# Adaptive average pooling on one core: the sum of each tile moved from GpSimd and VectorE to VectorE alone, and the last tile cut in two

## The chip, the cores and the metric

The kernel runs on one core of one Trainium2 chip. A core has engines that work side by side: VectorE (DVE in the profile), ScalarE (ACT), GpSimd (POOL), TensorE (PE, not used here) and SyncE (SP), which here only issues DMA transfers. Sixteen DMA engines move data between the memory (HBM) and the core's on-chip buffer of 128 partitions. The metric is the device time of one execution in microseconds (us). Before the change it is 333.39 us, the median of 3 runs (333.32 to 333.48).

## The reference

The input `x` is float32, 32 x 256 x 4096; the output is 32 x 256 x 256. With 4096 columns and 256 outputs every window has exactly 16 columns:

```python
for i in range(output_size):
    start = int(i * length / output_size)
    end = int((i + 1) * length / output_size)
    result[:, :, i] = np.mean(x[:, :, start:end], axis=-1)
```

So 8192 rows of 4096 numbers become 8192 rows of 256 means: 134.22 MB are read and 8.39 MB written, and there is one addition for each number read.

## The kernel before

The 8192 rows are worked in 16 tiles. A tile gives each of the 128 partitions 4 whole rows, 16384 numbers (64 KiB), in all 8.39 MB. `cells` = 1024 is the number of outputs of a tile in each partition, `cols` = 16384 the number of inputs, `window` = 16, and `m` = 512 is half of `cells`.

Tiles 0 to 14 are read from `x_many`, and their results stay on the chip in `res_many` until all 15 are there; one store of 7.86 MB then writes them. Tile 15 has its own source `x_last` and result `res_last`, which is written with two small stores: 120 partitions, then 8.

The input buffers come from `inpool`, which has two. The load of tile t can be issued only when tile t-2, which had the same buffer, has been summed. All DMA transfers are issued by SyncE, in the order of the program: SP's queue holds the 16 loads (L73), behind the last load the large store (L58 by way of `store`), then the two small stores. An instruction that waits on this queue holds back everything behind it.

For each tile the engines do this:

- L73: SyncE issues the load.
- L76: GpSimd adds, for the second half of the cells, the upper 8 columns of each window onto the lower 8, in place.
- L81: VectorE sums the first half of the cells, 16 columns for each (128 x 8192 numbers in, 128 x 512 out). It does not wait for GpSimd and runs beside it.
- L84: VectorE sums the second half of the cells, for which 8 columns are left (128 x 4096 in, 128 x 512 out). It waits for L76.
- L87: ScalarE multiplies the tile's 1024 results in place by 1/16.

The two buffers and the waits between the engines are handled by the framework's pool; the stores carry a semaphore of their own, on which SyncE waits at the end (L99).

Of the kernel before, what the change touches and what calls it, by code (L numbers as in the profile page):

```python
# [1 line left out]

# [4 lines left out]


@with_exitstack
def kernel(  # L10
    ctx: ExitStack,
    tc: tile.TileContext,
    x: bass.AP,
    output_size: int,
    out: bass.AP,
):

    nc = tc.nc
    F32 = mybir.dt.float32
    X = mybir.AxisListType.X

    batch, channels, length = x.shape
    ob, oc, olen = out.shape
    assert ob == batch and oc == channels and olen == output_size
    assert length % output_size == 0
    window = length // output_size  # L30
    hw = window // 2
    inv_w = 1.0 / float(window)

    P = nc.NUM_PARTITIONS
    R = 4
    rows = batch * channels
    assert rows % (P * R) == 0
    ntiles = rows // (P * R)
    many = (ntiles - 1) * R
    cells = R * output_size  # L40
    m = cells // 2
    cols = R * length

    xr = x.rearrange("b c l -> (b c) l")
    orow = out.rearrange("b c o -> (b c) o")
    x_many = xr[0 : P * many, :].rearrange("(p r) l -> p (r l)", p=P, r=many)
    o_many = orow[0 : P * many, :].rearrange("(p r) o -> p (r o)", p=P, r=many)
    x_last = xr[P * many :, :].rearrange("(p r) l -> p (r l)", p=P, r=R)
    o_last = orow[P * many :, :].rearrange("(p r) o -> p (r o)", p=P, r=R)

    res_many = nc.alloc_sbuf_tensor("res_many", [P, (ntiles - 1) * cells], F32, align_bytes=256)
    res_last = nc.alloc_sbuf_tensor("res_last", [P, cells], F32, align_bytes=256)
    inpool = ctx.enter_context(tc.tile_pool(name="inpool", bufs=2))

    stored = nc.alloc_semaphore("stored")

    def store(out, in_):
        ins = nc.sync.dma_start(out=out, in_=in_)  # L58
        tc.no_tile_sem_insts.add(ins.ins.name)
        ins.then_inc(stored, 16)  # L60

    for t in range(ntiles):
        last = t == ntiles - 1
        xbuf = inpool.tile([P, cols + 64], F32, name="xin")
        off = 32 if last else 0
        flat = xbuf[:, off : off + cols]
        xin = flat.rearrange("p (o w) -> p o w", w=window)
        if last:
            res, base, src = res_last, 0, x_last
        else:  # L70
            res, base = res_many, t * cells
            src = x_many[:, t * cols : (t + 1) * cols]
        nc.sync.dma_start(out=flat, in_=src)  # L73
        if last:
            store(o_many, res_many[:, :])
        nc.gpsimd.tensor_add(  # L76
            out=xin[:, m:cells, 0:hw],
            in0=xin[:, m:cells, 0:hw],
            in1=xin[:, m:cells, hw:window],
        )  # L80
        nc.vector.reduce_sum(  # L81
            out=res[:, base : base + m], in_=xin[:, 0:m, :], axis=X
        )
        nc.vector.reduce_sum(  # L84
            out=res[:, base + m : base + cells], in_=xin[:, m:cells, 0:hw], axis=X
        )
        nc.scalar.mul(  # L87
            out=res[:, base : base + cells],
            in_=res[:, base : base + cells],
            mul=inv_w,  # L90
        )
    for lo, hi in ((0, 120), (120, P)):
        store(o_last[lo:hi, :], res_last[lo:hi, :])

    ctx.pop_all().close()
    tc.close()
    tc.compile()  # L97
    nc.sync.wait_ge(stored, 48)
    nc.sync.sem_clear(stored)  # L99


# [1 line left out]
_INS = ['x', 'output_size']  # L103
_OUTS = [((32, 256, 256), 'float32')]

_NUMBERS = {'output_size': 256}


# [26 lines left out]
```

## Time and profile before

| | |
|---|---|
| median of 3 runs | 333.39 us |
| span of the profiled execution (first to last instruction) | 332.2 us |
| VectorE busy | 209.7 us, 63% |
| GpSimd busy | 139.7 us, 42% |
| ScalarE busy | 18.2 us, 5% |
| DMA packets' time, as a share of 16 engines' span | 99.4% |
| bytes moved | 142.61 MB, 429 GB/s over the span |
| GpSimd's add, 128x4096, each | 8719 ns |
| VectorE's sum, 128x8192, each | 8686 ns |
| VectorE's sum, 128x4096, each | 4420 ns |
| ScalarE's scaling, 128x1024, each | 1056 ns |

The profile records one execution, and its page gives the span from the first to the last instruction of that execution. It holds no other time of that execution; the median of the runs is 1.2 us above the span. "Landing" of a DMA transfer is the moment from which an engine that waits for its data can go on. A row of the timeline gives the start, the length, the engine, the line, the operation and its tile, and in brackets the idle time before it with what ended it. A row of the table of windows gives the window, its length, the busy time of VectorE, ScalarE and GpSimd with the number of instructions, TensorE's clock, the mean busy share of the DMA engines and their GB/s.

### The profile page before, as it was taken

What the parts mean: (1) busy time and instruction counts of PE and PEld (TensorE: products, weight loads), DVE (VectorE), ACT (ScalarE), POOL (GpSimd) and SP (SyncE); (2) the same over time, 40 slices, a digit from 0 to 9 for tenths busy, and PEclk for the clock granted to TensorE, in tenths of its full rate; (3) what the DMA queues carried; (4) which work ended last, traced back from release to release, by engine and by line L of the source; (5) the groups of instructions that cost most, each with busy time, mean ns of one, the idle gap of its engine ahead of it and who ended that gap; (6) DMA issues with size and microseconds to landing.
All of it is one profiled execution on the core that took longest, in us unless ns stands there. A gap on an engine that the chain in (4) does not pass through costs nothing.

```text
span 332.2 us, 160 instructions
## 1 busy us (share of the span) xinstructions
DVE 209.7 (63%) x32; ACT 18.2 (5%) x17; POOL 139.7 (42%) x20
## 2 busy tenths in 40 slices
DVE  0029396692939669392956939295683929578392
ACT  1000101000010100001010000101000010101001
POOL 0027090642709064370906337090633709063370
DMA  9898989989898999989898998989899998989897
GB/s 379 379 505 379 505 379 442 442 379 505 379 505 379 481 402 402 481 379 505 379 497 387 466 418 379 505 379 505 379 489 395 418 466 379 505 379 505 363 473 300
DMA packets 2599, 142.61 MB, mean 429 GB/s; under 512 B 295, under 2 KB 295, under 8 KB 423
## 3 DMA queue, kind: packets, MB, share of 16 engines
q1 hardware_dynamic: 2599, 142.61, 99.4%
HBM read 134.22 MB, written 8.39 MB: 429 GB/s over the span
## 4 chain that ended last, share of the span: by engine, by line
DMA 66%; POOL 18%; DVE 11%; POOLq 3%; issue 0%; ACT 0%; SPq 0%
DMA xin<-in_x_dram 66%; POOL xin L76 18%; DVE res_many L84 9%; POOLq L97 3%; DVE res_last L84 1%; ACT res_last L87 0%; SPq L73 0%; POOLq L76 0%
## 5 line engine op out<-in xcount | busy, mean ns | idle before, releaser
L76 POOL TENSOR_TENSOR xin<-xin 128x4096 f32<-128x4096 f32 x16 | 139.5, 8719 | 181.9 <-DMA xin<-in_x_dram 181.9
L81 DVE TENSOR_REDUCE res_many<-xin 128x512 f32<-128x8192 f32 x15 | 130.3, 8686 | 107.3 <-DMA xin<-in_x_dram 107.3
L84 DVE TENSOR_REDUCE res_many<-xin 128x512 f32<-128x4096 f32 x15 | 66.3, 4420 | 2.5 <-POOL xin L76 2.3
L87 ACT ACTIVATE res_many<-res_many 128x1024 f32<-128x1024 f32 x15 | 15.8, 1056 | 289.6 <-DVE res_many L84 289.6
L81 DVE TENSOR_REDUCE res_last<-xin 128x512 f32<-128x8192 f32 x1 | 8.7, 8686 | 6.6 <-DMA xin<-in_x_dram 6.6
L84 DVE TENSOR_REDUCE res_last<-xin 128x512 f32<-128x4096 f32 x1 | 4.4, 4420 | 0.2 <-POOL xin L76 0.2
L87 ACT ACTIVATE res_last<-res_last 128x1024 f32<-128x1024 f32 x1 | 1.1, 1056 | 18.8 <-DVE res_last L84 18.8
L87 ACT ACT_TABLE_LOAD x1 | 1.3, 1283 | 0.7 <-PEq L116 0.7
L116 POOL MEMSET const-float32-0.0<- 128x1 f32 x1 | 0.1, 99 | 0.2 <-issue 0.2
L116 POOL MEMSET const-bfloat16-1.0<- 128x1 bf16 x1 | 0.1, 102 | 0.0
L116 POOL MEMSET const-uint8-127<- 128x1 uint8 x1 | 0.1, 102 | 0.0
L116 POOL MEMSET const-float32-1.0<- 128x1 f32 x1 | 0.1, 99 | 0.0
## 6 DMA issues: line engine op xcount, KB each, us to landing
out_dram<-res_many SPq DMA_DIRECT2D x1, 7680.0 KB
out_dram<-res_last SPq DMA_DIRECT2D x1, 480.0 KB
xin<-in_x_dram SPq DMA_DIRECT2D x16, 25.3
out_dram<-res_last SPq DMA_DIRECT2D x1, 32.0 KB
```

Source lines behind the costliest of these rows:

```text
L76: nc.gpsimd.tensor_add(out=xin[:, m:cells, 0:hw], in0=xin[:, m:cells, 0:hw], in1=xin[:, m:cells, hw:window],)
L81: nc.vector.reduce_sum(out=res[:, base : base + m], in_=xin[:, 0:m, :], axis=X)
L84: nc.vector.reduce_sum(out=res[:, base + m : base + cells], in_=xin[:, m:cells, 0:hw], axis=X)
L87: nc.scalar.mul(out=res[:, base : base + cells], in_=res[:, base : base + cells], mul=inv_w,)
L97: tc.compile()
L116: nc = _bacc.Bacc("TRN2", target_bir_lowering=False, num_devices=1)
```

## The change

GpSimd's add (L76) is removed. Each tile is summed by one instruction of VectorE over all 1024 cells with 16 columns each, and scaled by one instruction of ScalarE as before. The last tile is treated as two column halves (`parts` = 2): two loads of 128 x 8192 numbers one after the other on SP's queue, each with its own sum and its own scaling. The large store is still issued behind the loads of the last tile, and the small stores at the end.

```diff
+    def sums(xin, res, base, count):
+        nc.vector.reduce_sum(out=res[:, base : base + count], in_=xin, axis=X)
+        nc.scalar.mul(
+            out=res[:, base : base + count],
+            in_=res[:, base : base + count],
+            mul=inv_w,
+        )
+
     for t in range(ntiles):
...
         if last:
-            res, base, src = res_last, 0, x_last
+            res, base, src, parts = res_last, 0, x_last, 2
         else:
-            res, base = res_many, t * cells
+            res, base, parts = res_many, t * cells, 1
             src = x_many[:, t * cols : (t + 1) * cols]
-        nc.sync.dma_start(out=flat, in_=src)
+        pc, pm = cols // parts, cells // parts
+        for k in range(parts):
+            nc.sync.dma_start(
+                out=flat[:, k * pc : (k + 1) * pc], in_=src[:, k * pc : (k + 1) * pc]
+            )
         if last:
             store(o_many, res_many[:, :])
-        nc.gpsimd.tensor_add(
-            out=xin[:, m:cells, 0:hw],
-            in0=xin[:, m:cells, 0:hw],
-            in1=xin[:, m:cells, hw:window],
-        )
-        nc.vector.reduce_sum(
-            out=res[:, base : base + m], in_=xin[:, 0:m, :], axis=X
-        )
-        nc.vector.reduce_sum(
-            out=res[:, base + m : base + cells], in_=xin[:, m:cells, 0:hw], axis=X
-        )
-        nc.scalar.mul(
-            out=res[:, base : base + cells],
-            in_=res[:, base : base + cells],
-            mul=inv_w,
-        )
+        xin = flat.rearrange("p (o w) -> p o w", w=window)
+        for k in range(parts):
+            sums(xin[:, k * pm : (k + 1) * pm, :], res, base + k * pm, pm)
```

More of the change, by code (lines that the diff above doesn't have):

```diff
@@ L30 @@
     window = length // output_size
-    hw = window // 2
     inv_w = 1.0 / float(window)
@@ L40 @@
     cells = R * output_size
-    m = cells // 2
     cols = R * length
@@ L66 @@
         flat = xbuf[:, off : off + cols]
-        xin = flat.rearrange("p (o w) -> p o w", w=window)
         if last:
-            res, base, src = res_last, 0, x_last
+            res, base, src, parts = res_last, 0, x_last, 2
         else:
-            res, base = res_many, t * cells
+            res, base, parts = res_many, t * cells, 1
             src = x_many[:, t * cols : (t + 1) * cols]
-        nc.sync.dma_start(out=flat, in_=src)
+        pc, pm = cols // parts, cells // parts
[3 more added lines that the diff above has]
+            )
         if last:
             store(o_many, res_many[:, :])
-        nc.gpsimd.tensor_add(
-            out=xin[:, m:cells, 0:hw],
-            in0=xin[:, m:cells, 0:hw],
-            in1=xin[:, m:cells, hw:window],
-        )
-        nc.vector.reduce_sum(
-            out=res[:, base : base + m], in_=xin[:, 0:m, :], axis=X
-        )
-        nc.vector.reduce_sum(
-            out=res[:, base + m : base + cells], in_=xin[:, m:cells, 0:hw], axis=X
-        )
-        nc.scalar.mul(
-            out=res[:, base : base + cells],
-            in_=res[:, base : base + cells],
-            mul=inv_w,
-        )
+        xin = flat.rearrange("p (o w) -> p o w", w=window)
+        for k in range(parts):
+            sums(xin[:, k * pm : (k + 1) * pm, :], res, base + k * pm, pm)
     for lo, hi in ((0, 120), (120, P)):
```

## The prediction

> **What bounds the kernel now.** I read the busy and DMA shares of the page first, then the chain that ended last, then the load line, then windows and the timeline at both ends.
>
> Page, parts 1 to 3:
>
> ```profile
> DVE 209.7 (63%) x32; ACT 18.2 (5%) x17; POOL 139.7 (42%) x20
> ...
> DMA  9898989989898999989898998989899998989897
> ...
> q1 hardware_dynamic: 2599, 142.61, 99.4%
> ```
>
> No engine is near full, the 16 DMA engines are: their packets fill 99.4% of the span. The kernel is bound by moving 142.61 MB, and any change can only lose by making the DMA engines wait, or win a little where the transfers start and end.
>
> The chain, two tiles of its middle (start, length, what):
>
> ```profile
> 80.68 8.73 POOL xin L76
> 89.41 0.02 issue
> 89.43 4.43 DVE res_many L84
> 93.86 0.02 issue
> 93.88 25.29 DMA xin<-in_x_dram
> 119.17 0.03 issue
> ```
>
> This is the circuit of one of the two input buffers: landed, summed (13.3 us), reload issued, 25.3 us to landing. It closes every 38.6 us, in which two tiles land. It does not show who is the bound: of the 25.3 us a part is waiting behind the other buffer's load. That is in the load line's times to landing:
>
> ```profile
> L73 SPq DMA_DIRECT2D xin<-in_x_dram x16: 327/328/420, 0.7 to 287.1; - x16
> ...
> DMA to landing us min/median/max: 21.8/25.3/40.6
> ```
>
> 21.8 us is the first load, which found idle queues; the median queued behind another. In the timeline two landings are one load's transfer apart: VectorE starts at 273.78 and 293.08, 19.30 us, 8.39 MB at 434 GB/s. So an unqueued load is 19.3 us of transfer and about 2.5 us of start and landing, and the median waits 25.3 - 21.8 = 3.5 us behind its neighbour. That 3.5 us is what the kernel has to spare per buffer circuit.
>
> The end, from the timeline and a table of windows:
>
> ```profile
> 293.08 8.69 DVE L81 TENSOR_REDUCE res_many<-xin 128x512 f32<-128x8192 f32 x1 [6.02 <-DMA xin<-in_x_dram]
> ...
> 306.40 1.06 ACT L87 ACTIVATE res_many<-res_many 128x1024 f32<-128x1024 f32 x1 [18.25 <-DVE res_many L84]
> 307.48 0.35 SPq L58 DMA_DIRECT2D out_dram<-res_many  x1
> 312.96 8.69 DVE L81 TENSOR_REDUCE res_last<-xin 128x512 f32<-128x8192 f32 x1 [6.59 <-DMA xin<-in_x_dram]
> ```
>
> ```profile
> 326.27 1.06 ACT L87 ACTIVATE res_last<-res_last 128x1024 f32<-128x1024 f32 x1 [18.81 <-DVE res_last L84]
> 327.35 0.74 SPq L58 DMA_DIRECT2D out_dram<-res_last  x2
> ```
>
> ```profile
> 1.17:22.16 20.99, 0.00 (x0) 0.84 (x1) 0.00 (x0) 1.00 1.06 446
> ...
> 60.84:292.76 231.92, 157.26 (x24) 12.67 (x12) 104.62 (x12) 1.00 1.00 434
> 292.76:312.56 19.80, 13.11 (x2) 1.06 (x1) 8.72 (x1) 1.00 1.00 421
> 312.56:330.20 17.64, 13.11 (x2) 1.06 (x1) 8.72 (x1) 1.00 0.91 394
> ```
>
> The large store (7.86 MB, 18.1 us at 434 GB/s) is issued 5 us before the last load is through and follows it without a gap; the last tile's arithmetic ends at 327.33 under that store. The end too is transfer time.
>
> **The change part by part.**
>
> *GpSimd's add goes.* 16 instructions of 8.72 us (POOL). In each tile it stands between landing and VectorE's second sum.
>
> *VectorE sums the tile whole.* The two rows give the price: 128x8192 takes 8686 ns, 128x4096 takes 4420 ns, so 4096 more elements cost 4266 ns (1.042 ns each) over a fixed 154 ns. 16384 elements: 154 + 17064 = 17.22 us. Bounds: 17.06 without a fixed part, 17.37 by doubling the 8686 row. The 8686 row ran beside GpSimd and the 4420 row did not, and one line goes through both with a small fixed part, so I see nothing for VectorE to gain from GpSimd's absence. VectorE goes from 209.7 to about 276 us, 83% of the span, still under the 19.3 us per tile.
>
> *The buffer circuit.* From landing to reload issued: before 13.3 us (50.63 + 4.43 less the start at 41.83, and 0.02), after 17.22 + 0.03 = 17.25 us. That takes 3.9 or 4.0 us out of a reserve of 3.5 us. In full: a reload issued 17.25 us after landing, and landing 21.8 us after its issue if its start is like the first load's, closes the circuit in 39.05 us. Two transfers need 38.6. The longer one sets the pace: +0.4 us for two tiles. The circuit is run through seven times by each buffer from the first landings to tiles 14 and 15, and both buffers' circuits run at the same time: 7 x 0.4 = 2.9 us. The first load's issue took 0.40 us on SP's queue, the later ones 0.33; with that 0.07 taken off, 7 x 0.34 = 2.4 us. I take 2.4.
>
> The unknown is what a reload costs that arrives when the DMA engines are just running dry, since before none did. From below: nothing, if its start lies beside the neighbour's last packets. The nearest fact on that is this table of the first load's start:
>
> ```profile
> 1.13:1.70 0.57, 0.00 (x0) 0.57 (x1) 0.00 (x0) 1.00 0.00 0
> 1.70:2.20 0.50, 0.00 (x0) 0.31 (x1) 0.00 (x0) 1.00 5.83 1966
> ```
>
> The last two columns are the DMA engines' busy share and GB/s. Packets are counted where they start: 1966 GB/s in 0.5 us are 15 packets of 65,536 bytes, so 15 of 16 DMA engines start within 1.0 to 1.4 us of the issue at 0.73. But in the packet records those first packets last about 3.05 us and all later ones 2.418, so the pipe also fills for some 0.6 us; that the fill hides behind a neighbour's packet is open. From above: the whole 21.8 us with a sum of 17.37 us, 7 x 0.56 = 3.9 us. I take the first load's row because it is the same transfer, queue and tile; only its neighbour differs.
>
> *The last tile's two halves.* Two loads of 4.19 MB in place of one; the second is issued some 0.35 us behind the first on SP's queue and transfers behind it, so it adds nothing. SP's order is kept: both loads, then the large store, which waits for ScalarE on tile 14. That wait grows: tile 14 lands at 293.08, is summed at 310.30, scaled (1.06 us) at 311.4; the store is issued at 311.4 in place of 307.48. Before, the 5 us of load still queued covered its start. Now the last load's transfer ends at about 312.1 to 312.6 and the store's bytes start at 311.4 plus between 1.0 us (the table above) and 2.1 us (21.8 less 19.3 of transfer less 0.4 from the last packet to VectorE's start): 312.4 to 313.5 against 312.6 before, or -0.1 to +0.9. I take +0.7, near the upper end, since the store meets empty queues, like the first load. What waits behind it on SP's queue are the two small stores.
>
> *The last sums.* VectorE is now late: tile 14 until 310.3, then two halves of 8.69 us until 327.7 (both halves landed long before). ScalarE on 128x512 is between half of 1.06 and all of it; say 0.6. The small stores are issued at 328.4, 1.0 later than before. The large store covers this: with its 18.1 us it now ends at about 331, and 328.4 + 2.1 = 330.5. If it started at 312.4 the cover would be gone and the small stores would add up to 0.1. Stall shifts both alike.
>
> *GpSimd's queue* loses its waits; no one else waited for it. ACT gets one instruction more, at the end, counted above.
>
> **The sum.** The profiled span is 332.2; the median of the runs, 333.39, lies 1.2 above it, which I keep as what lies around the span. 332.2 + 2.4 + 0.7 = 335.3, plus 1.2: 336.5 us. Of the DMA engines' time, the 3.1 us are new gaps.
>
> **The rivals.**
>
> *The reload's start is hidden anyway.* If a reload only has to be issued some 1.4 us before the neighbour ends, 17.25 + 1.4 + 19.3 + 0.4 = 38.35 is under 38.6 and the pace stays 19.3 per tile. Only the store's late start is left: 333.39 - 0.1 to + 0.9, so 333.3 to 334.3, 334.0 at my value. For it: descriptors reach 15 of 16 engines in that time. Against it: the long first packets, and the one engine whose first packet starts at 2.84. The Trainium skill, DMA: Bandwidth & Descriptors, Anatomy of one DMA, fits a fixed 2.0 us plus bytes at 436 GB/s, for GpSimd-issued DMAs: 21.2 us for this load by estimate, against the 21.8 measured here on SP's queue. By it the circuit is 38.5 us, just inside the two transfers, and this rival would hold, with a time of 334.0. The measured row outweighs it, but the difference is only 0.6 us in 39.
>
> *The reload starts later than the first load did*, because the queues and the memory are busy. At 1 us more, the circuit is 40 us and the loss 7 x 1.4 = 9.8: with the store's 0.7, 343.9 us. For it: the first load had the memory to itself. Against it: nothing here shows a start under load that takes longer; the issue itself gets shorter, 0.33 for 0.40.
>
> *Faster: the transfers speed up without GpSimd's reads and writes of the tile.* The price is the load's 19.3 us. The window of the first load, without any engine at work, has 446 GB/s against 434 later; at that rate a load is 18.8. It decides only where the circuit follows: 17.25 + start + 18.8 must be under 38.6, so a start under 2.55 us, which the first load's 2.5 barely meets; with a start of 1.4 the two transfers bind at 37.6 and the kernel gains 7 x 1.0, less 0.7: 327.1 us. Against it: the 446 comes from counting packets where they start, and packets last 2.418 us with and without GpSimd at work.
>
> **How the numbers follow.** Two runs of this kernel can be told apart by about 0.2%, 0.67 us. Start not hidden, as summed: 0.65, 334.3 to 338.4 (the lower end for a stall of 0.1 us a circuit, the upper for 3.9 us of stall and 0.9 at the store with 0.2 for the rest). Hidden: 0.23, 333.3 to 334.3, of which about 0.13 lies within 0.67 us of 333.39. Later start: 0.08. Faster: 0.04. Range 333.6 to 338.5, which leaves out the last two and the lowest part of the second. Slower: 0.65 + 0.10 + 0.08 = 0.83; same 0.13; faster 0.04.
>
> **What would show it.** Sums of 128x16384 at 17.2 us; time from load to landing with a median near 21.8 instead of 25.3; VectorE starts 19.5 us apart from tile to tile; VectorE waiting about 2.3 us for each load; DMA share below 99% in the middle; the store issued near 314; the small stores still not on the path. Starts 19.3 apart with a DMA share of 1.00 in the middle would show the first rival; starts 20 apart or more the second; starts below 19.2 the third. The prediction is wrong if a reload's start overlaps its neighbour's last packets, or if the sum is not linear in its elements.

## The result, and the profile after

The changed kernel takes 349.94 us (median of 4 runs, 348.85 to 352.37) against 333.44 us for the kernel before on the same chip: 1.050 times as long, 95% interval 1.048 to 1.053. Forecast were 336.5 us and at most 338.5. The sign was right, the size was five times too small.

The profiled execution took 352.37 us and has a span of 351.1 us, 18.9 us more than the span of before; it is the slowest of the four, and the medians differ by 16.5 us. From its page, the busy times, the DMA engines' digits, the queue and the sums:

```profile
DVE 275.5 (78%) x17; ACT 18.4 (5%) x18; POOL 0.2 (0%) x4
...
DMA  8989999997999899989989899898989979999995
...
q1 hardware_dynamic: 2743, 142.61, 96.1%
...
L61 DVE TENSOR_REDUCE res_many<-xin 128x1024 f32<-128x16384 f32 x15 | 258.3, 17220 | 67.9 <-DMA xin<-in_x_dram 67.9
```

A whole sum takes 17.22 us, as worked out. VectorE is still no bound: it waits 67.9 us for loads. But the DMA engines, with the same bytes, fell from 99.4% to 96.1%. They have gaps, and the chain of work that ended last shows where (start, length, what):

```profile
39.73 24.16 DMA xin<-in_x_dram
63.89 0.02 issue
63.91 17.23 DVE res_many L61
81.14 0.02 issue
81.16 24.20 DMA xin<-in_x_dram
...
122.64 23.86 DMA xin<-in_x_dram
...
163.77 22.05 DMA xin<-in_x_dram
...
203.09 24.66 DMA xin<-in_x_dram
...
245.02 24.55 DMA xin<-in_x_dram
...
286.84 22.09 DMA xin<-in_x_dram
```

The chain now goes round one buffer without any part hidden: sum 17.25 us, reload, sum. Two reloads took about the 21.8 us from issue to landing that the prediction used. The other five took 23.9 to 24.7. Before, such numbers cost nothing since they held 3.5 us of waiting behind the other buffer's load. Here most engines have next to nothing to wait for: by the packet records the first DMA engine through with the other load ran dry, that is, had no packet left to move, 1.3 us after the issue at the latest, in four of the seven cases before it. (The records hold the start, length and size of each packet of the trace, but not its engine. Which engine went on or stood empty is inferred from packets that start where another ends.)

From VectorE's start on tile 0 to its start on tile 14, the seven circuits add up to 308.95 - 22.48 = 286.5 us, against 293.08 - 22.53 = 270.6 before: 15.9 us lost. The other 3.0 of the 18.9 us lie behind tile 14 (351.1 - 308.95 = 42.1, before 332.2 - 293.08 = 39.1). The stores there:

```profile
327.29 0.35 SPq L56 DMA_DIRECT2D out_dram<-res_many  x1
...
344.05 1.62 SPq L56 DMA_DIRECT2D out_dram<-res_last  x2
```

What a slow reload looks like is seen in windows around the one issued at 39.73, and for comparison around the quick one issued at 163.77 (start, length, busy times, TensorE's clock, DMA share, GB/s; packets are counted where they start, one packet has 65,536 bytes):

```profile
41.16:41.70 0.54, 0.00 (x0) 0.00 (x0) 0.00 (x0) 1.00 2.70 1092
41.70:42.50 0.80, 0.69 (x1) 0.00 (x0) 0.00 (x0) 1.00 0.20 82
42.50:43.70 1.20, 1.20 (x1) 0.00 (x0) 0.00 (x0) 1.00 0.76 273
164.72:165.10 0.38, 0.00 (x0) 0.11 (x1) 0.00 (x0) 1.00 7.78 2587
```

In the last row 15 packets (2587 GB/s x 0.38 us) start 0.95 to 1.33 us after the issue, on 15 DMA engines which by the packet records had all run dry before the issue. In the first three rows 9, 1 and 5 packets start (the sixteenth just ahead of them, at 41.16); the last five come 2.8 to 3.9 us after the issue. At that issue all 16 engines were still at the other load's last packets, and ran dry 1.3 to 1.75 us after it. Eight went on without a gap, the others stood empty, the last one for over 2 us. The reload issued at 81.16 shows both kinds at once. Eleven engines ran dry within 0.3 us of its issue, before or after it; they got their first packets 0.97 to 1.33 us after the issue. The other five were busy until 1.25 to 1.75 us after it; one of them went on at once, and four got their first packets 2.8 to 3.5 us after it (11, 1 and 4 packets in the rows):

```profile
82.10:82.50 0.40, 0.00 (x0) 0.12 (x1) 0.00 (x0) 1.00 5.44 1802
82.50:83.50 1.00, 0.23 (x1) 0.00 (x0) 0.00 (x0) 1.00 0.18 66
83.50:84.70 1.20, 1.20 (x1) 0.00 (x0) 0.00 (x0) 1.00 0.65 218
```

A load has landed when its last engine is done, so the latest of 16 sets VectorE's start and with it the next issue. The reload issued at 245.02 shows it: 15 engines went on without a gap and were done by 266.3, one got its first packet 4.5 us after the issue and was done at 269.26, and the load landed at 269.57.

A late engine is also handed on. The slowest reload of the chain, the one issued at 203.09 (24.66 us), started on 15 engines within 2.0 us. The sixteenth was still busy until 207.5 with the other buffer's load, which had itself been started there 3.8 us after its issue, and went on with the new load at once. So one of the five slow circuits waited for a late start of its neighbour, not for one of its own.

### The profile page after: what moved, and what is told of

It reads as the page before. It is cut to its first block, busy times and chain, and to the rows that moved or that the text cites. A ratio compares the mean times of both kernels' runs of the same rounds, so it can differ in the third digit from the quotient of the medians.

```text
span 351.1 us, 115 instructions
## 1 busy us (share of the span) xinstructions
DVE 275.5 (78%) x17; ACT 18.4 (5%) x18; POOL 0.2 (0%) x4
## 3 DMA queue, kind: packets, MB, share of 16 engines
q1 hardware_dynamic: 2743, 142.61, 96.1%
## 4 chain that ended last, share of the span: by engine, by line
DMA 53%; DVE 42%; DVEq 2%; ACT 0%; issue 0%
DMA xin<-in_x_dram 53%; DVE res_many L61 39%; DVEq L93 2%; DVE res_last L61 2%; ACT res_last L62 0%
## 5 line engine op out<-in xcount | busy, mean ns | idle before, releaser
L61 DVE TENSOR_REDUCE res_many<-xin 128x1024 f32<-128x16384 f32 x15 | 258.3, 17220 | 67.9 <-DMA xin<-in_x_dram 67.9
L61 DVE TENSOR_REDUCE res_last<-xin 128x512 f32<-128x8192 f32 x2 | 17.3, 8676 | 0.0
L62 ACT ACTIVATE res_last<-res_last 128x512 f32<-128x512 f32 x2 | 1.3, 630 | 15.5 <-DVE res_last L61 15.5
## 6 DMA issues: line engine op xcount, KB each, us to landing
xin<-in_x_dram SPq DMA_DIRECT2D x15, 24.2
```

What stands on the lines that cost most here:

```text
L61: nc.vector.reduce_sum(out=res[:, base : base + count], in_=xin, axis=X)
L62: nc.scalar.mul(out=res[:, base : base + count], in_=res[:, base : base + count], mul=inv_w,)
```

## The experiments

All times stand against the kernel before, run beside them on the same chip (333.4 to 333.5 us).

### Which part of the change: the cut last tile, or GpSimd's absence

`e1_halves_only` keeps GpSimd for tiles 0 to 14 and takes over only the two halves of the last tile:

```diff
+        if last:
+            for k in range(parts):
+                sums(xin[:, k * pm : (k + 1) * pm, :], res, base + k * pm, pm)
+            continue
         nc.gpsimd.tensor_add(
```

> Tiles 0 to 14 as before, with GpSimd; only the last tile is loaded, summed and scaled in two halves by VectorE. Late-start theory (the loss arises where a reload is issued too close to the moment when the DMA engines run dry): no loss in the middle, the last two loads are issued 13.3 us after landing as before, so 333.4 to 334.0 us; VectorE's last sum ends near 328 under the large store. Rival, the cut last tile is the cause: near 350 us, or at least several us above 333.4.

`e2_whole_last` leaves GpSimd out and keeps the last tile whole:

```diff
-            res, base, src, parts = res_last, 0, x_last, 2
+            res, base, src, parts = res_last, 0, x_last, 1
```

> GpSimd left out, the last tile loaded and summed whole. Late-start theory: the middle as in the changed kernel, 7 circuits of about 2.3 us loss each, so 349 to 352 us. Rival, the cut last tile is the cause: near 334 us.

Measured: halves alone 333.47 us (ratio 0.9999, interval 0.999 to 1.0009); GpSimd left out alone 351.65 us (1.0535, 1.0518 to 1.0553). All of the loss comes with leaving out GpSimd in tiles 0 to 14. Whether it is the longer hold of the buffer or GpSimd's absence as such, the next kernels separate. The halves did move the last sums forward, as the timeline of the first of these kernels shows:

```profile
306.52 17.27 DVE L63 TENSOR_REDUCE res_last<-xin 128x512 f32<-128x8192 f32 x2
...
324.48 0.97 SPq L58 DMA_DIRECT2D out_dram<-res_last  x2
```

The small stores are issued at 324.48 in place of 327.35, and the time is the same: by the packet records the engines are through with the large store at 330.1 to 330.7 in both kernels, and the small stores wait behind it either way.

### How the loss grows with the hold of a buffer

Three kernels give GpSimd a smaller part of the cells, so that VectorE sums more of each tile whole. Only `m` is changed:

```diff
-    m = cells // 2
+    m = cells - cells // 4
```

(and `// 8`, `// 16`).

> GpSimd halves a quarter of the cells instead of a half; a buffer is free 15.3 us after landing (13.3 before, 17.25 changed). First-load theory of the prediction (21.8 us from issue to landing): circuit 37.1 us, under the 38.6 of two transfers, no loss: 333.4. Late theory A, any reload under load takes 24.2 us: circuit 39.5, loss 7 x 0.85 = 6 us: 339 us. Late theory B, only DMA engines that have run dry pay for the start, and a reload reaches the others within some 1.7 us: the reload comes 3.2 to 3.7 us before the DMA engines run dry, no loss: 333.4.

> GpSimd halves an eighth of the cells; a buffer is free 16.35 us after landing, the reload comes 2.1 to 2.6 us before the DMA engines run dry. First-load theory: circuit 38.15, no loss: 333.4 to 334. Late theory A (24.2 us always): circuit 40.55, loss 7 x 1.9 = 13 us: 347 us. Late theory B (only engines run dry pay): no loss in the middle, 333.4 to 334.5.

> GpSimd halves a sixteenth of the cells; a buffer is free 16.9 us after landing. Slow-hand-over theory (a reload reaches idle DMA engines within 1 to 2 us, busy ones up to 4 us after its issue, and the last of the 16 sets the landing): between the eighth (343.6) and the changed kernel (350 to 352): 345 to 350 us. Any theory with a sharp threshold between 16.35 and 17.25 us that explains only the changed kernel is already excluded by the eighth; if this run lies below 343, the loss does not grow with the release time and the theory falls.

| kernel | buffer held, us | time, us | ratio, 95% interval | median issue to landing, us |
|---|---|---|---|---|
| before | 13.3 | 333.5 | | 25.3 |
| a quarter | 15.2 | 334.31 | 1.0031 (1.0017 to 1.0044) | 23.6 |
| an eighth | 16.3 | 343.56 | 1.0315 (1.0287 to 1.0342) | 23.4 |
| a sixteenth | 16.8 | 345.39 | 1.0350 (1.0334 to 1.0366) | 23.7 |
| changed | 17.25 | 349.94 | 1.0504 (1.0478 to 1.053) | 24.2 |

By the prediction's price for a reload (21.8 us) the eighth's circuit would be 38.1 us, under the 38.6 of two transfers, and cost nothing. It costs 10 us. The medians in the last column hold the wait behind the other load too. What counts is the sum with the hold: 38.6, 38.8, 39.7, 40.5 and 41.5 us, against 38.6 for two transfers. Not all of each loss lies in the circuits: from VectorE's start on tile 0 to its start on tile 14 the profiled executions lose 1.1, 7.1, 10.5 and 15.9 us. The rest lies behind that, and in the three kernels that keep GpSimd the small stores have a part in it: after a longer last sum they are issued only about when the large store ends (at 330.18 in the quarter, where the engines end it between 330.4 and 331.7).

Theory A, 24.2 us for every reload, gave 339 and 347: too much for both. Theory B, that only engines that have run dry pay and the others are reached in 1.7 us, gave 333.4 for the quarter and at most 334.5 for the eighth, which refutes it: its first reloads were issued 2 us before the engines ran dry. The sixteenth lies in the band that was given for it, at its lower end. The truth lies between the two theories, and the chain of the quarter shows how narrow it gets there:

```profile
57.25 23.89 DMA xin<-in_x_dram
81.14 0.02 issue
81.17 12.95 DVE res_many L81
94.12 2.20 DVE res_many L84
96.32 0.02 issue
96.34 23.44 DMA xin<-in_x_dram
```

15.2 + 23.9 = 39.1 us for the first circuit shown, 0.5 over two transfers, where 21.8 us would have left 1.6 us to spare. It is the longest of the chain; the next one closes in 38.6. In the packet records of the quarter the engines begin to run dry 2.5 to 3.1 us after a reload's issue, and still a few of them stand empty, with first packets 2.9 to 4.1 us after the issue. So a reload that is issued less than about 3 us ahead can already lose.

It need not: in the sixteenth the first two reloads, issued at 39.37 and 58.67, came 1.7 to 2.2 us before the engines ran dry, went on without a gap on all 16 and landed after 21.84 and 21.85 us. The third, issued at 78.00 with the same lead, found ten engines empty until 2.5 to 3.1 us after the issue and landed after 23.41 us. The lead alone does not tell which reload will be late.

### Is it the start from dry engines

`e5_one_buffer` has one input buffer; each reload meets DMA engines that have been idle for 17 us:

```diff
-    inpool = ctx.enter_context(tc.tile_pool(name="inpool", bufs=2))
+    inpool = ctx.enter_context(tc.tile_pool(name="inpool", bufs=1))
```

> The changed kernel with one input buffer: every reload is issued when all DMA engines have been idle for 17 us. If a start from idle engines is as short as the first load's, each load lands about 21.8 us after its issue, a tile takes 39.05 us, and the last tile with the store behind it brings the whole to about 15 x 39 + 22 + 17 + 20 = 645 us. If only the very first load is quick and every later start is slow (24.2 us), a tile takes 41.4 us and the whole about 680 us.

Measured: 631.58 us (one run). The load line's times to landing (the shortest is a half of the last tile):

```profile
L80 SPq DMA_DIRECT2D xin<-in_x_dram x17: 327/328/427, 0.7 to 588.0; - x17
...
DMA to landing us min/median/max: 12.0/21.9/22.8
```

and the start of the reload issued at 79.11:

```profile
79.11:80.00 0.89, 0.00 (x0) 0.88 (x1) 0.00 (x0) 1.00 0.00 0
80.00:80.50 0.50, 0.00 (x0) 0.18 (x1) 0.00 (x0) 1.00 6.02 1966
80.50:81.10 0.60, 0.00 (x0) 0.00 (x0) 0.00 (x0) 1.00 0.25 109
```

15 packets start within 1.4 us and the last within 2.0, much as for the first load (1.4 and 2.1). So 21.8 us was the right price for a reload that finds all engines idle, not a privilege of the first load. Starting from dry engines is not what makes a reload late; being issued to engines that are about to run dry, but still busy, can. (The expected 645 us was 13 too long: the large store follows the last loads at once, and the last sums, which the 645 had as 17 us of their own, run beside it.)

### Does the lateness last as long as a packet

`e6_packets16` sets the rows of a tile 64 bytes apart in the buffer, so that packets have 16 KB:

```diff
-        flat = xbuf[:, off : off + cols]
+        rowed = xbuf.rearrange("p (r l) -> p r l", r=R)[:, :, 0:length]
```

> The changed kernel with the four rows of a tile 64 bytes apart in the buffer, so that a load goes in packets of 16 KB instead of 64 KB; same sums, same issue times. If a reload's start on a DMA engine is late because it waits for something as long as a packet (one of 64 KB lasts 2.42 us), the late starts shrink from up to 3.9 us after the issue to some 2 us, and the time falls to 334 to 340 us. If the lateness has nothing to do with the packets' length, the time stays at 346 to 352 us.

Measured: 350.44 us (1.0497, 1.0456 to 1.0537), the same loss, with 8759 packets instead of 2743. On one queue, then, the late start is not a wait for a packet in progress. The median from issue to landing is 24.0 us.

### With the same sums but reloads issued early

`e7_four_half` has tiles of half the size and four buffers, so the same bytes on the chip, and VectorE alone:

```diff
-    R = 4
+    R = 2
...
-    inpool = ctx.enter_context(tc.tile_pool(name="inpool", bufs=2))
+    inpool = ctx.enter_context(tc.tile_pool(name="inpool", bufs=4))
```

> VectorE alone as in the changed kernel, but tiles of 2 rows for each partition (4.19 MB) and four buffers: the same bytes on the chip. A reload is issued 8.7 us after its landing, with two to three other loads (9.66 us each) ahead of it. Late-start theory: the reload comes some 20 us before the DMA engines run dry, no loss; the large store is issued earlier and the last store is half as long: 332.5 to 333.6 us. Rival, VectorE's long reads or GpSimd's absence slow the transfers: near 350 us.

`e9_four_half_early` also stores most of the results behind the last loads without a wait:

```diff
-            store(o_many, res_many[:, :])
+            early = (ntiles - 5) * cells
+            store(o_many[:, 0:early], res_many[:, 0:early])
+            store(o_many[:, early:], res_many[:, early:])
```

> VectorE alone with four half-size buffers, and the large store in two parts: the results of tiles 0 to 26 are stored behind the last loads without a wait, tiles 27 to 30 behind that. If the 2.3 us that the four-buffer kernel lost to the kernel before lie at the start of its large store (issued when the loads had just ended), they go: 332.8 to 333.7 us. If they lie elsewhere (33 loads instead of 16, the smaller packets), it stays at 335.5 to 336.

Measured: 335.85 us (1.0071, 1.0058 to 1.0083) and 334.16 us (1.0021, 1.0011 to 1.003). Both missed the bands: the first lies 2.3 us above its own and far under the rival's 350, the second between the two that were given. The first in a window from its first tile to its last:

```profile
12.67:312.83 300.16, 269.96 (x32) 19.50 (x31) 0.00 (x0) 1.00 1.00 432
```

The middle has no gap, with VectorE busy for 270 of 300 us and GpSimd unused. So neither VectorE's long reads nor GpSimd's absence slows the transfers; the circuit does. The 2.3 us that were left lie at the end, on the timeline of the same kernel:

```profile
303.45 8.69 DVE L61 TENSOR_REDUCE res_many<-xin 128x512 f32<-128x8192 f32 x1 [1.00 <-DMA xin<-in_x_dram]
...
312.82 0.34 SPq L56 DMA_DIRECT2D out_dram<-res_many  x1
```

The store is issued at the moment in which the last load ends (by the packet records 312.83), and its start lies open: its first packets come 0.85 to 1.0 us after the issue. Storing 27 of 31 tiles' results without that wait gave back 1.7 of the 2.3 us. The last 0.7 us to the kernel before are not accounted for. No version tried here beats the kernel before.

### Two queues

`e8_two_queues` issues the odd tiles' loads from ScalarE's queue:

```diff
-            nc.sync.dma_start(
+            (nc.scalar if t % 2 else nc.sync).dma_start(
```

> The changed kernel with the odd tiles' loads issued from ScalarE's queue. If the lateness comes from a reload being handed over on a queue whose last packets are just ending, a second queue removes it for most loads: 334 to 340 us. If it comes from the DMA engines being busy, whatever the queue, or from the start of a dry engine, it stays at 346 to 353 us.

Measured: 373.0 us (1.1185, 1.1168 to 1.1202), outside both expectations. The time could not answer the question, because the second queue turned the order of the loads upside down. The timeline:

```profile
42.00 34.35 DVE L61 TENSOR_REDUCE res_many<-xin 128x1024 f32<-128x16384 f32 x2 [42.00 <-DMA xin<-in_x_dram]
59.25 42.02 SPq L80 DMA_DIRECT2D xin<-in_x_dram  x2
...
76.39 0.33 ACTq L80 DMA_DIRECT2D xin<-in_x_dram  x1
83.69 34.34 DVE L61 TENSOR_REDUCE res_many<-xin 128x1024 f32<-128x16384 f32 x2 [7.35 <-DMA xin<-in_x_dram]
```

Tile 0 lands only at 42.0, in place of 22.5, and VectorE then sums two tiles back to back: the loads of the two queues share the DMA engines and land together. On one queue the first load is through before the second begins, which is what makes two buffers overlap with the sums. The Trainium skill, DMA: Bandwidth & Descriptors, Queues, rings and completion order, says that a DMA engine takes turns between queues packet by packet. The 42.0 us agree with that.

The packet records of this kernel, which name the queue, answer more than its time. From the third load on, SP's reloads met engines that had nothing to do, and their first packets start 0.95 to 2.0 us after the issue. ScalarE's reloads met engines that were all busy with SP's load, on a queue of their own that was empty. In all seven cases their first packets start 3.7 to 4.5 us after the issue (the last tile's is the first of its two halves), on every one of the 16 engines, and each engine started one more packet of SP's load in between, 1.3 to 2.1 us after the issue. ScalarE's queue as such is not slow: its first load, issued at 0.73 to idle engines, started after 1.0 to 1.65 us. So the late start does not need a queue whose own last packets are ending; a busy engine is enough. Whether the new load reached the engines only after that one packet had started, or waited its turn behind it, the records do not tell.

## Why the prediction was wrong

- *What bounds the kernel, and the reserve of 3.5 us in a buffer's circuit:* right. The change took 3.95 us (17.25 for 13.3), and the circuit now sets the pace in place of the transfers.
- *The sum in one instruction:* 17.22 us forecast, 17.22 measured. GpSimd's absence neither helped nor hurt VectorE or the transfers (`e7_four_half`).
- *The price of a reload:* this is the step that failed. "I take the first load's row because it is the same transfer, queue and tile; only its neighbour differs." The neighbour is what counts. 21.8 us holds when the engines are idle (`e5_one_buffer`, 21.9; two of seven circuits here, 22.05 and 22.09, in which 15 of 16 engines were idle). When several are at their last packets, it was 23.9 to 24.7 us in five of seven circuits, one of them by a late engine inherited from the neighbour. The upper bound of 3.9 us for all seven was taken from the same row, so the range could not hold it: 15.9 us were lost, where 2.4 were forecast. (That 2.4 also has a slip: 39.05 less 38.6 is 0.45, so that seven circuits make 3.2, and 2.7 after the 0.07 is taken off. The 0.3 us do not matter here.)
- *The rivals:* the second one, a reload that starts later under load, was the case, with 2.1 to 2.9 us more in place of the 1 us it was priced with; its reason, busy queues and memory, is not shown beyond the busy engines. It was given 0.08 because nothing in the profile showed a slow start under load. Nothing showed a quick one either: before, each reload had 5 us of queue ahead of it. An unseen price should not have been bounded by its most favourable sighting.
- *The first rival, a hidden start,* falls with the same runs; the measured circuits were 39.3 to 41.9 us. With it falls the estimate of 38.5 us, which rested on the Trainium skill, DMA: Bandwidth & Descriptors, Anatomy of one DMA.
- *The store's late start, +0.7 us:* the stretch behind tile 14 grew by 3.0 us. The large store was issued at 327.29, but by the packet records the last load's engines ended between 327.9 and 331.1, where before they ended within 0.6 us of each other (312.0 to 312.6). Most of the 3.0 is that last slow reload again: 14 engines ended by 328.25, the store's first packets came 0.86 to 1.15 us after its issue on them, and the last engine went on at 331.13 without a gap. What an uncovered start of the store costs is not measured here by itself; in the four-buffer pair, where all engines had run dry, storing early gave back 1.7 us, more than the 0.7 taken. (The lower end of the term, 312.4 against 312.6, is -0.2 and not -0.1.)
- *The last sums and small stores:* forecast to stay under the large store. They do, in `e1_halves_only` and here: issued at 344.05, while by the packet records the first engine was through with the large store at 346.3.

What stays open is why a busy engine gets its new load up to 4.5 us after the issue when an idle one gets it after 1 to 2, and why on one queue this befalls some engines and not others. The issue on SP's queue takes the same 0.33 us in both, packets of a quarter of the length change nothing, and a queue of its own does not help. The Trainium skill, DMA: Bandwidth & Descriptors, Latency and other measured facts, puts the memory's access time at 0.2 us on average and 2 us under high load, which is near the size of the difference; no run here separates the memory from the hand-over of the load to the engines.

## What to carry to other kernels

A buffer's circuit (landing, use, reload, landing) has to be shorter than the transfers of all buffers together, and the reload in it must be priced as one that meets busy DMA engines: here about 24 us from issue to landing instead of 22. Keep the reload's issue some 5 us ahead of the moment when the queue runs dry, which cost nothing here where 2.5 to 3.1 us already lost a little, by holding buffers for a shorter time or by more and smaller ones; this kernel, at 99.4% of its DMA time, lost 5% by 4 us more of hold. Take a duration that the profile shows only for the idle start of a program as a lower bound for the same step under load.

## What was not expected of the hardware

- From issue to first packet: 0.95 to 2.1 us on idle engines, up to 4.5 us on engines just finishing another load of the same queue, on some of the 16 and not on others; 3.7 to 4.5 us on all 16 when they were busy with another queue's load. As the last engine sets the landing, one late engine can cost the whole load its delay, and the next load too.
- The loss has no sharp threshold: 0.3% at 15.2 us of hold, 3.2% at 16.3, 3.5% at 16.8, 5.0% at 17.25.
- Loads on two queues land together: the first at 42.0 us instead of 22.5.
